# Cosine attention on one core: fourteen pairs of heads turned by transfers, a sixth key chunk off ScalarE, twelve K scalings on VectorE

## The chip, the cores and the metric

The kernel runs on one core of one Trainium2 chip. The metric is the device time of one execution in microseconds, the median of several executions. The engines are TensorE (PE in the profile, its weight loads PEld), VectorE (DVE), ScalarE (ACT), GpSimd (POOL) and SyncE (SP, which here only issues transfers). Each runs its own list of instructions in order, and waits on semaphores.

## The reference

```python
# batch 8, heads 12, seq 512, dim 64, float32; tau 0.1
Q_norm = Q / (norm(Q, axis=-1) + 1e-10)
K_norm = K / (norm(K, axis=-1) + 1e-10)
scores = einsum('bhqd,bhkd->bhqk', Q_norm, K_norm) / tau
weights = exp(scores - max(scores));  weights /= sum(weights)
out = einsum('bhqk,bhkd->bhqd', weights, V)
```

The kernel needs no maximum: the scores of normalised rows lie between -10 and 10.

## The kernel before, in words

The 96 heads are worked off as 48 pairs. A pair's Q, K and V are 256 KB each. The steps of pair s, by the names in the code (a step's name is also its key in the program's table):

- LD and LV load Q, K and V (SP issues them); VC casts V to bf16 (GpSimd).
- SQ squares (GpSimd), SSQ and RED sum the squares of K (TensorE, then VectorE); BN and RED(s,0) take the statistics of Q on VectorE. NEW works out the reciprocal roots, for a group of up to four pairs at once (pairs 36 to 39, 40 to 43 and 44 to 47 are such groups).
- SCL(s,0) scales Q on VectorE, SCL(s,1) scales K: on GpSimd, or on VectorE for the pairs in `K_ON_DVE`. Result: tile qn, bf16, 128x512 each.
- TR(s,0), TR(s,1) turn Q and K on TensorE, four 128x128 transposes each, into the bank tps; EVA copies both to qt on VectorE.
- SCO(s,c) makes the scores of key chunk c (128 keys, both heads, two matmuls 64x128 by 64x512) in one half of the bank set scps. EXP(s,c) on ScalarE makes the weights of the chunk, 128x1024, one instruction. So a chunk's scores can be made when the exponential two chunks earlier has ended.
- PV(s,h,i) multiplies weights and V for head h and query block i (four matmuls). RCP and NRM divide by the sums on VectorE (one NRM of 128x512 for a pair, two of 128x256 for pairs with an off chunk and the last ones), ST stores. PV of the next pair writes the bank that NRM reads, so it waits for that NRM.

Five chunks have no exponential on ScalarE, the "off" chunks of the table `OFF`: chunk 3 of pairs 25, 33, 40 and 44, and chunk 2 of pair 47. Theirs is a polynomial: SCX(s,h) makes the scores of head h (one matmul) in the bank tps, X(s,h,0) and X(s,h,1) on VectorE read them into xp and xz, and Y(s,0) to Y(s,4), five steps on GpSimd, give the weights. There is one bank, so SCX(s,1) waits for X(s,0,1); there is one set of xp, xz and xw, so the next off chunk's X waits for the last Y of this one.

Rings of buffers: 15 for Q and K, 10 for V, 4 for qn, 4 for qt, 4 for the weights, 8 for the output.

The order of the work on each engine is written out in the table `ORDER` (from line 883): a list of numbers for each engine, each number the place of a step in the order in which the program was made up. Nothing is moved at run time; a step that waits holds up all that stands behind it on its engine. The waits themselves come from the needs that each step names.

The code has a second way of turning Q and K, used for pairs from `TURN_FROM` on: TD(s), one transposing transfer from qn to qt for Q and K together (line 555), issued by SP. It needs both scalings of the pair, and the scores of pair s-4, whose qt it overwrites. With `TURN_FROM = 99` no pair has it.

Of the kernel before, what the change touches and what calls it, by code (L numbers as in the profile page):

```python
# [5 lines left out]
ALU = mybir.AluOpType  # L6
# [103 lines left out]
def bass_cosine_similarity_attention_kernel(  # L110
# [10 lines left out]
    NT = SEQ // 128  # L121
# [48 lines left out]
    P = Program(nc)  # L170
# [179 lines left out]
    def pair(s):  # L350
# [164 lines left out]
        for w in range(2):  # L515
# [29 lines left out]
            def tr(e, w=w):  # L545
                for t in range(NT):
# [5 lines left out]
                  [("SCL", s, w), *(([("EVA", s - 1, 0)] if s - 1 in BY_HEAD else evas(s - 1)) if s > 1 else [("EVA", 0, 0, 0), ("EVA", 0, 0, 1)]), "eye"]  # L552
                  + [freed(*u) for u in turn_user.get(s - 1, [])[-1:]], tr)
# [21 lines left out]
    def turned(s):  # L575
        return s >= TURN_FROM

    last_eva = min(TURN_FROM, NP) - 1

# [32 lines left out]
    def freed(s, h):  # L612
        return ("Y", s, h, 3) if in_psum(s) else ("X", s, h, 1)

    def poly(s, c, at):
# [6 lines left out]
        for h in range(2):  # L622
            users = turn_user[turns[h]]
            before = [freed(*users[users.index((s, h)) - 1])] if users.index((s, h)) else []
            if turns[h] is None:
                before += [("SCL", i, w) for i in range(NP - 12, NP) for w in range(2)]
            elif prev:
                before.append(freed(prev[-1], 1))

            def sco(e, h=h):  # L630
# [3 lines left out]
            P.add(("SCX", s, h), "pe", "sco1", at + h, [*evas(s), *evas(min(turns[0], last_eva))] + before, sco)  # L634
            lift = LIFT_P if here else LIFT
            b_ps = x_ps if turns[h] is not None else nx_ps
            P.add(("X", s, h, 0), "dve", "x1", at + h, [("SCX", s, h)] + (exps(held[-1], off_of[held[-1]]) if held and not here else []),
# [3 lines left out]
                  (lambda e, h=h, b_ps=b_ps: e.scalar_tensor_tensor(out=yz[:, h, :], in0=b_ps, scalar=lift * UNIT - a0, in1=y_low[h], op0=ALU.add, op1=ALU.subtract)) if here else  # L641
                  (lambda e, h=h: e.scalar_tensor_tensor(out=xz[:, h, :], in0=xp[:, h, :], scalar=a0 - lift * UNIT, in1=x_ps, op0=ALU.add, op1=ALU.subtract)))  # L642
            if not here:
# [3 lines left out]
                      lambda e, h=h, b_ps=b_ps: e.scalar_tensor_tensor(out=et[s % R_ET][:, c, h, :], in0=yz[:, h, :], scalar=a1, in1=b_ps, op0=ALU.add, op1=ALU.mult)]  # L647
            for j, (step, need) in enumerate(zip(halves, ([("X", s, h, 1)] + [("Y", i, 4) for i in held[-1:]] + [cast_of(i) for i in range(NP - 8, NP)], [("Y", s, i, 1) for i in range(2)],
                                                          [("Y", s, h, 2)] + [key("PV", s - R_ET, i, NT - 1) for i in range(2)]))):
                P.add(("Y", s, h, j + 1), "pool" if j == 1 else "dve", "sqp" if j == 1 else "x1", at + 2 + 0.5 * h + 0.8 * j, need, step)  # L650
# [162 lines left out]
OFF = {(25, 3): (25, 25), (33, 3): (33, 33), (40, 3): (40, 40), (44, 3): (44, 44), (47, 2): (47, None)}  # L813
# [19 lines left out]
TURN_FROM = 99  # L833
# [4 lines left out]
OFF_ON_POOL = ((25, 3), (33, 3), (40, 3), (44, 3), (47, 2))  # L838
OFF_ON_BOTH = ()
X_ON_POOL = ()  # L840
K_ON_DVE = (1, 2, 3, 4, 9)
# [33 lines left out]
def slack(s, most):  # L875
# [133 lines left out]
```

## Time and profile before

| | |
|---|---|
| median of 3 runs | 185.53 us (185.46 to 185.81) |
| the profiled execution | 185.63 us, span from first to last instruction 183.9 us |
| granted TensorE clock | 1.000 |
| busy: TensorE, VectorE, ScalarE, GpSimd | 173.0, 172.9, 176.9, 163.8 us |
| the 16 DMA engines | full until about 124 us, when the last loads land; then stores alone |

How to read the rows: a group has line, engine, operation, output<-input, shapes and count, then the busy time in us, the mean of one in ns, and the idle time of the engine just before them with what ended it. A timeline row has start, duration, engine, line, operation, and in brackets an idle time before it. A windows row has the stretch, its length, and the busy us (with instruction counts) of PE, PEld, DVE, ACT and POOL, then the clock, the DMA share and GB/s. The durations of neighbouring VectorE or ScalarE instructions overlap a little, so what one costs its engine is the distance from its start to the next one's.

Lines: L538 is SCL, L547 TR, L570 EVA, L413 BN and the Q half of RED, L435 SSQ, L692 SCO, L716 and L707 EXP, L631 SCX, L639 and L642 X, L656, L657 and L662 Y, L741 and L778 PV, L760 and L789 RCP, L762 and L791 NRM, L725 VC.

### The profile page before, as it was taken

The page shows a single profiled execution, that of the slowest core. Times are in us where ns is not written, and L with a number is a line of the kernel's source. Part 1 is how long each engine was busy: PE and PEld are TensorE (multiplying, and loading weights), DVE is VectorE, ACT ScalarE, POOL GpSimd, SP SyncE. Part 2 cuts the span into 40 slices and gives each one's busy share as a digit, 9 for nine tenths or more (in the row PEclk, how much of TensorE's full clock was granted, in tenths as well). Part 3 has the DMA queues.
Part 4 walks back from the last instruction along what each step waited for, and adds up shares of the span by engine and source line. Part 5 has one row for each costly group of instructions (what it writes and reads, how often), then busy time and mean ns, then how long its engine had stood idle before and what let it go on. Part 6 is the DMA issues. An engine that isn't in the chain of part 4 may idle for free.

```text
span 183.9 us, 6826 instructions
## 1 busy us (share of the span) xinstructions
PE 173.0 (94%) x2738; PEld 109.9 (60%) x2738; DVE 172.9 (94%) x622; ACT 176.9 (96%) x205; POOL 163.8 (89%) x153
## 2 busy tenths in 40 slices
PE   7989999999999999999999899999899999899993
PEld 2546666657666666666755566656466656556562
DVE  2799999999999999999999999999999999997995
ACT  5799999999999999999999999999999999999992
POOL 4699999839989999996999999999999999998960
PEclk9999999999999999999999999999999999999999
DMA  5999999999999999999999999995115213013134
GB/s 162 331 356 346 349 350 356 380 375 384 379 376 377 379 383 379 383 378 375 357 372 383 370 383 380 377 323 190 61 59 193 96 62 114 5 65 110 57 132 157
DMA packets 52479, 50.77 MB, mean 276 GB/s; under 512 B 3296, under 2 KB 52448, under 8 KB 52448
## 3 DMA queue, kind: packets, MB, share of 16 engines
q1 hardware_dynamic: 52016, 50.05, 79.8%
q8 instruction: 21, 0.34, 0.8%
q10 hardware_dynamic: 432, 0.30, 0.5%
q14 instruction: 10, 0.08, 0.1%
HBM read 37.75 MB, written 12.58 MB: 274 GB/s over the span
## 4 chain that ended last, share of the span: by engine, by line
ACT 69%; DVE 11%; PE 10%; POOL 5%; issue 2%; DMA 1%; POOLq 1%; DVEq 0%
ACT et L716 68%; PE oops L741 3%; PE scps L692 3%; POOL xw L657 2%; DVE ob L762 2%; DVE qn L538 1%; PE tps L547 1%; DMA qk<-in_Q_dram 1%; DVE qt L570 1%; POOL et L657 1%; DVE xp L639 1%; PE oops L435 1%; DVE xs L284 1%; DVE xz L642 1%; DVE et L647 1%
## 5 line engine op out<-in xcount | busy, mean ns | idle before, releaser
L716 ACT ACTIVATE et<-scps 128x1024 bf16<-128x1024 f32 (+1 forms) x188 | 171.1, 1073 | 1.3 <-PE scps L692 1.2
L692 PE MATMUL scps<-qt 64*128 64x512 bf16 x374 | 73.7, 386 | 4.5 <-ACT et L716 3.6
L741 PE MATMUL oops<-vb,et 128*128 128x65 bf16 x1504 | 70.3, 194 | 0.9 <-DVE ob L762 0.8
L741 PEld LDWEIGHTS oops<-vb,et 128*128 128x128 bf16 x1504 | 54.5, 97 | 26.4 <-issue 16.0
L538 POOL TENSOR_TENSOR qn<-qk,rk 128x512 bf16<-128x512 f32 x42 | 43.5, 1043 | 7.4 <-DVE rk L482 4.1
L538 DVE TENSOR_TENSOR qn<-qk,nps 128x512 bf16<-128x512 f32 x52 | 34.7, 678 | 0.6 <-ACT nps L474 0.6
L394 POOL TENSOR_TENSOR sq<-qk 128x512 bf16<-128x512 f32 x34 | 34.9, 1040 | 0.0
L762 DVE TENSOR_TENSOR ob<-oops,rd 128x256 f32<-128x256 f32 (+1 forms) x64 | 34.3, 542 | 0.3
L547 PE MATMUL tps<-ident,qn 128*128 128x128 bf16 x376 | 32.5, 220 | 0.6 <-DVE qn L538 0.3
L570 DVE COPY qt<-tps 128x1024 bf16<-128x1024 bf16 x47 | 32.0, 681 | 0.8 <-PE tps L547 0.7
L413 DVE BATCH_NORM_STATS2 st<-qk 128x6 f32<-128x128 f32 x136 | 31.7, 282 | 0.0
L692 PEld LDWEIGHTS scps<-qt 64*128 64x128 bf16 x374 | 18.0, 92 | 21.1 <-ACT et L716 8.5
L547 PEld LDWEIGHTS tps<-ident,qn 128*128 128x128 bf16 x376 | 21.4, 98 | 11.6 <-issue 5.2
L725 POOL TENSOR_SCALAR vb<-vf 128x1024 bf16<-128x1024 f32 (+1 forms) x29 | 26.2, 910 | 0.3
L397 POOL TENSOR_TENSOR sq<-qk 128x1024 bf16<-128x1024 f32 x10 | 18.8, 1893 | 0.1
L435 PE MATMUL oops<-sq,ident 128*128 128x64 bf16 x320 | 16.0, 193 | 0.0
L435 PEld LDWEIGHTS oops<-sq,ident 128*128 128x128 bf16 x320 | 11.9, 98 | 4.1 <-issue 3.1
L760 DVE RECIPROCAL rd<-oops 128x4 f32<-128x4 f32 (+1 forms) x64 | 11.4, 186 | 1.0 <-PE oops L741 0.4
L657 POOL TENSOR_TENSOR xw<-xw,xz 128x1024 f32<-128x1024 f32 x4 | 9.4, 2358 | 0.3
L657 POOL TENSOR_TENSOR et<-xw,xp 128x1024 bf16<-128x1024 f32 x4 | 8.5, 2133 | 0.2
L448 DVE TENSOR_REDUCE nps<-oops 128x8 f32<-128x64 f32 x38 | 8.1, 213 | 0.1
L657 POOL TENSOR_TENSOR xw<-xz 128x1024 f32<-128x1024 f32 x4 | 7.6, 1893 | 0.7 <-DVE xz L642 0.7
(76 smaller groups left out, 111.4 us busy)
## 6 DMA issues: line engine op xcount, KB each, us to landing
vf<-in_V_dram SPq DMA_DIRECT2D x48, 256.0 KB, 6.4
out_dram<-ob SPq DMA_DIRECT2D x47, 256.0 KB, 6.3
qk<-in_Q_dram SPq DMA_DIRECT2D x46, 256.0 KB, 6.4
qk<-in_K_dram SPq DMA_DIRECT2D x46, 256.0 KB, 6.5
qk<-in_Q_dram SPq DMA_DIRECT2D x4, 128.0 KB, 3.0
qk<-in_K_dram ACTq DMA_DIRECT2D x2, 128.0 KB, 2.8
qk<-in_K_dram SPq DMA_DIRECT2D x2, 128.0 KB, 3.2
out_dram<-ob SPq DMA_DIRECT2D x1, 128.0 KB, 1.7
```

What stands on the lines that cost most here:

```text
L394: lambda e: e.tensor_tensor(out=sqf[:, 8 * DIM :], in0=data[:, 8 * DIM :], in1=data[:, 8 * DIM :], op=ALU.mult))
L413: last = e.bn_stats(out=st[:, g % R_X, c8 + 4 * h + t : c8 + 4 * h + t + 2, :].rearrange("p g x -> p (g x)"), in_=rows[:, t : t + 2].rearr ...
L435: last = e.matmul(out=o_ps[bank][:, at : at + 64], lhsT=ident[:, :], rhs=sq[iqs][:, 8 * w : 8 * w + 8, 8 * k : 8 * k + 8], start=(k == 0), ...
L538: lambda e, w=w, r=r: e.tensor_tensor(out=qn[iqn][:, w].rearrange("p t h d -> p h t d"), in0=qk[iq][:, w].rearrange("p h (t d) -> p h t d" ...
L547: last = e.transpose(t_ps[:, w, t, :], qn[iqn][:, w, t].rearrange("p h d -> p (h d)"), ident[:, :])
L570: lambda e, ws=ws: e.tensor_copy(out=qt[iqt][:, ws, :, :].rearrange("p w t x -> p (w t x)"), in_=t_ps[:, ws, :, :].rearrange("p w t x -> p ...
L657: mul = lambda o, x, y: lambda e: e.tensor_tensor(out=o, in0=x, in1=y, op=ALU.mult)
L692: last = e.matmul(out=sc_ps[:, 2 * b + h, :], lhsT=qt[iqt][64 * h : 64 * h + 64, 1, c, :], rhs=qt[iqt][64 * h : 64 * h + 64, 0, :, :], sta ...
L716: lambda e, c=c, b=b, hs=hs: e.activation(out=et[iet][:, c, hs[0] : hs[-1] + 1, :], in_=sc_ps[:, 2 * b + hs[0] : 2 * b + hs[-1] + 1, :], f ...
L725: return e.tensor_scalar(out=vb[:, ib // 2, :, ib % 2 : ib % 2 + n, :, 0:DIM].rearrange("p c r h d -> p (r h) c d"), in0=vf[:, iv : iv + n ...
L741: last = e.matmul(out=o_ps[h][:, 65 * t : 65 * t + 65], lhsT=et[iet][:, c, h, 128 * t : 128 * t + 128], rhs=vb[:, s % R_VB // 2, c, s % 2, ...
L762: lambda e, hs=hs, grid=grid: e.tensor_tensor(out=ob[io][:, hs], in0=grid[:, :, :, 0:DIM], in1=rd[io][:, hs, :].unsqueeze(3).to_broadcast( ...
```

## The change

- `TURN` names the pairs 34 to 47: their TR and EVA steps are gone (28 and 14), and 14 transposing transfers TD stand in SP's list.
- `OFF` has a sixth chunk, (38, 3), its polynomial on GpSimd: one EXP less, two SCX, four X and five Y more; pair 38's RCP and NRM come in two halves, and the scales of its group are made for the polynomial.
- `K_ON_DVE` has pairs 36 to 47 more: twelve SCL(s,1) go from GpSimd to VectorE. All pairs of their groups are then on VectorE, so NEW needs no step more.
- The needs are written for any set of turned pairs (`eva_by`); an off chunk's SCX waits for the last EVA before it. A variant `IN_PLACE` is added and empty.
- The orders of SP, GpSimd, VectorE and TensorE are new from about pair 12 on; ScalarE's loses EXP(38,3).

```diff
+            P.add(("TR", s, w), "pe", "tr", T0 - PERIOD + 0.9 * TR_AT[w],
+                  [("SCL", s, w), *(([("EVA", s - 1, 0)] if s - 1 in BY_HEAD else evas(eva_by(s - 1))) if s > 1 else [("EVA", 0, 0, 0), ("EVA", 0, 0, 1)]), "eye"]
...
     def turned(s):
-        return s >= TURN_FROM
+        return s in TURN
-    last_eva = min(TURN_FROM, NP) - 1
+    last_eva = max(s for s in range(NP) if not turned(s))
+    def eva_by(s):
+        return max(i for i in range(s + 1) if not turned(i))
...
-            P.add(("SCX", s, h), "pe", "sco1", at + h, [*evas(s), *evas(min(turns[0], last_eva))] + before, sco)
+            P.add(("SCX", s, h), "pe", "sco1", at + h, [*evas(s), *evas(eva_by(turns[0]))] + before, sco)
...
-OFF = {(25, 3): (25, 25), (33, 3): (33, 33), (40, 3): (40, 40), (44, 3): (44, 44), (47, 2): (47, None)}
+OFF = {(25, 3): (25, 25), (33, 3): (33, 33), (38, 3): (38, 38), (40, 3): (40, 40), (44, 3): (44, 44), (47, 2): (47, None)}
-TURN_FROM = 99
+IN_PLACE = ()
+TURN = tuple(range(34, 48))
 TURN_AT = 10
-OFF_ON_POOL = ((25, 3), (33, 3), (40, 3), (44, 3), (47, 2))
+OFF_ON_POOL = ((25, 3), (33, 3), (38, 3), (40, 3), (44, 3), (47, 2))
-K_ON_DVE = (1, 2, 3, 4, 9)
+K_ON_DVE = (1, 2, 3, 4, 9, 36, 37, 38, 39, 40, 41, 42, 43, 44, 45, 46, 47)
```

The parts of the new lists that the text below speaks of, with the numbers resolved into names:

```
TensorE  ... SCO(35,2) SCO(35,3) SCX(38,0) PV(34,0,0) PV(34,0,1) PV(34,0,2) PV(34,1,0) PV(34,0,3) PV(34,1,1)
         PV(34,1,2) SSQ(42,1) PV(34,1,3) SCX(38,1) SCO(36,0) SCO(36,1) PV(35,0,0) ...
         ... PV(40,0,2) PV(40,0,3) SCO(43,0) ...     (PV(40,h,3) needs Y(40,4))
         ... PV(47,2,2) PV(47,2,3) PV(47,1,3) PV(47,0,0) PV(47,0,1) PV(47,0,2) PV(47,0,3)
VectorE  ... SCL(38,0) SCL(38,1) BN(42) SCL(36,1) NEW RCP(32) RED(40,1) NRM(32) SCL(36,0) SCL(39,0) SCL(37,1)
         SCL(37,0) NEW RCP(33,1) RCP(33,0) RED(41,1) NRM(33,0) NRM(33,1) X(38,0,0) X(38,0,1) RCP(34)
         RED(42,1) NRM(34) X(38,1,0) NEW X(38,1,1) ...
         ... NRM(37) X(40,0,0) NEW X(40,0,1) SCL(42,1) X(40,1,0) RCP(38,0) RED(46,1) X(40,1,1) ...
GpSimd   ... Y(38,0) to Y(38,4) SQ(47) VC(40) Y(40,0) to Y(40,4) VC(42) VC(44) VC(46) Y(44,0) to Y(44,4) ...
SP       ... LV(44) TD(34) TD(35) LV(41) TD(38) TD(36) TD(37) ST(28) ST(30) ST(32) TD(39) TD(40) TD(41)
         LV(40) LV(46) TD(42) LV(47) LV(45) ST(31) ST(34) TD(43) LV(43) TD(44) ST(36) LV(42) TD(45) ...
```

In TensorE's list before, two of pair 34's PV stand ahead of SCO(35,3), four between it and SCO(36,0), and two with the SSQ behind that.

More of the change, by code (lines that the diff above doesn't have):

```diff
@@ L551, in pair @@
             P.add(("TR", s, w), "pe", "tr", T0 - PERIOD + 0.9 * TR_AT[w],
-                  [("SCL", s, w), *(([("EVA", s - 1, 0)] if s - 1 in BY_HEAD else evas(s - 1)) if s > 1 else [("EVA", 0, 0, 0), ("EVA", 0, 0, 1)]), "eye"]
-                  + [freed(*u) for u in turn_user.get(s - 1, [])[-1:]], tr)
+                  [("SCL", s, w), *(([("EVA", s - 1, 0)] if s - 1 in BY_HEAD else evas(eva_by(s - 1))) if s > 1 else [("EVA", 0, 0, 0), ("EVA", 0, 0, 1)]), "eye"]
+                  + [freed(*u) for i in range(eva_by(s - 1), s) for u in turn_user.get(i, [])[-1:]], tr)
         if turned(s):
@@ L627, in poly @@
             elif prev:
-                before.append(freed(prev[-1], 1))
+                before.append(freed(prev[-1], max(i for i in range(2) if OFF[prev[-1], off_of[prev[-1]]][i] is not None)))
             def sco(e, h=h):
@@ L632, in sco @@
                                 rhs=qt[s % R_QT][64 * h : 64 * h + 64, 0, :, :], start=True, stop=True)
-            P.add(("SCX", s, h), "pe", "sco1", at + h, [*evas(s), *evas(min(turns[0], last_eva))] + before, sco)
+            P.add(("SCX", s, h), "pe", "sco1", at + h, [*evas(s), *evas(eva_by(turns[0]))] + before, sco)
             lift = LIFT_P if here else LIFT
             b_ps = x_ps if turns[h] is not None else nx_ps
-            P.add(("X", s, h, 0), "dve", "x1", at + h, [("SCX", s, h)] + (exps(held[-1], off_of[held[-1]]) if held and not here else []),
+            P.add(("X", s, h, 0), "dve", "x1", at + h, [("SCX", s, h)] + [("Y", i, h, 3) for i in prev if here and in_psum(i)] + (exps(held[-1], off_of[held[-1]]) if held and not here else []),
                   (lambda e, h=h, b_ps=b_ps: e.tensor_scalar(out=yp[:, h, :], in0=b_ps, scalar1=-MIDDLE, scalar2=BIG + lift * UNIT, op0=ALU.add, op1=ALU.add)) if here else
@@ L640, in poly @@
             P.add(("X", s, h, 1), "dve", "x1", at + h, [("X", s, h, 0)],
-                  (lambda e, h=h, b_ps=b_ps: e.scalar_tensor_tensor(out=yz[:, h, :], in0=b_ps, scalar=lift * UNIT - a0, in1=y_low[h], op0=ALU.add, op1=ALU.subtract)) if here else
+                  (lambda e, h=h, b_ps=b_ps: e.scalar_tensor_tensor(out=b_ps if s in IN_PLACE else yz[:, h, :], in0=b_ps, scalar=lift * UNIT - a0, in1=y_low[h], op0=ALU.add, op1=ALU.subtract)) if here else
                   (lambda e, h=h: e.scalar_tensor_tensor(out=xz[:, h, :], in0=xp[:, h, :], scalar=a0 - lift * UNIT, in1=x_ps, op0=ALU.add, op1=ALU.subtract)))
@@ L647, in poly @@
                       lambda e, h=h, b_ps=b_ps: e.scalar_tensor_tensor(out=et[s % R_ET][:, c, h, :], in0=yz[:, h, :], scalar=a1, in1=b_ps, op0=ALU.add, op1=ALU.mult)]
+            if s in IN_PLACE:
+                halves = [lambda e, h=h, b_ps=b_ps: e.tensor_tensor(out=yz[:, h, :], in0=b_ps, in1=b_ps, op=ALU.mult),
+                          lambda e, h=h, b_ps=b_ps: e.scalar_tensor_tensor(out=b_ps, in0=b_ps, scalar=-a2, in1=y_two[h], op0=ALU.add, op1=ALU.mult),
+                          halves[2]]
+                for j, (step, need) in enumerate(zip(halves, ([("X", s, h, 1)], [("Y", s, h, 1)], [("Y", s, h, 2)] + [key("PV", s - R_ET, i, NT - 1) for i in range(2)]))):
+                    P.add(("Y", s, h, j + 1), "dve" if j else "pool", "x1" if j else "sqp", at + 2 + 0.5 * h + 0.8 * j, need, step)
+                continue
             for j, (step, need) in enumerate(zip(halves, ([("X", s, h, 1)] + [("Y", i, 4) for i in held[-1:]] + [cast_of(i) for i in range(NP - 8, NP)], [("Y", s, i, 1) for i in range(2)],
```

109 rows, old and new, of the table ORDER are left out of this document.

## The prediction

> **What bounds the kernel now.** I read the page's busy times and slices first, then the chain, then the groups with shapes kept apart, then the timelines of single engines from 126 us on, where the change lies.
>
> ```profile
> span 183.9 us, 6826 instructions
> PE 173.0 (94%) x2738; PEld 109.9 (60%) x2738; DVE 172.9 (94%) x622; ACT 176.9 (96%) x205; POOL 163.8 (89%) x153
> ...
> DVE  2799999999999999999999999999999999997995
> ACT  5799999999999999999999999999999999999992
> ...
> 9.09 124.45 ACT et L716 x137
> ...
> L716 ACT ACTIVATE et<-scps 128x1024 bf16<-128x1024 f32 x184 | 169.1, 1084 | 0.1
> L538 POOL TENSOR_TENSOR qn<-qk,rk 128x512 bf16<-128x512 f32 x42 | 43.5, 1043 | 7.4 <-DVE rk L482 4.1 <-DVE nps L482 3.2
> L538 DVE TENSOR_TENSOR qn<-qk,nps 128x512 bf16<-128x512 f32 x52 | 34.7, 678 | 0.6 <-ACT nps L474 0.6
> L547 PE MATMUL tps<-ident,qn 128*128 128x128 bf16 x376 | 32.5, 220 | 0.6 <-DVE qn L538 0.3 <-DVE xz L642 0.3
> L570 DVE COPY qt<-tps 128x1024 bf16<-128x1024 bf16 x47 | 32.0, 681 | 0.8 <-PE tps L547 0.7
> ```
>
> ScalarE is the bound: its exponentials idle 0.1 us in all, and the chain stays on them from 9 us to 133 us. One costs 169.1/184 = 0.92 us. But VectorE is nearly as full. From where the two orders part (VectorE's list, pair 12's normalising at about 59 us) to 136 us:
>
> ```profile
> 58.00:136.00 78.00, 74.78 (x1227) 47.84 (x1227) 77.63 (x291) 78.00 (x86) 74.42 (x67) 1.00 0.97 334
> ```
>
> The third busy time is VectorE: 77.63 of 78.00 us. An order that gives it more to do before some point reaches that point later by all of it but 0.37 us. So each edit has two questions: does ScalarE lose an instruction, and what must VectorE have done when ScalarE's next scores are due?
>
> **The change part by part.**
>
> *Pair 38's sixth chunk leaves ScalarE:* one 128x1024 exponential less, -0.92 us, if nothing makes ScalarE wait.
>
> *Q and K of pairs 34 to 47 turned by transfers:* off TensorE go 14x8 transposes (0.55 to 0.59 us a pair), which gain nothing by themselves, as TensorE is not the bound; off VectorE go 14 copies (L570).
>
> *K of pairs 36 to 47 scaled on VectorE:* 12 scalings of 1043 ns leave GpSimd and come to VectorE. GpSimd gets pair 38's five polynomial steps (8.7 us, below), so it ends about 4 us lighter. VectorE's costs, by the starts of neighbours, since their durations overlap:
>
> ```profile
> 133.16 0.68 DVE L762 TENSOR_TENSOR ob<-oops,rd 128x512 f32<-128x512 f32 x1
> 133.76 0.68 DVE L538 TENSOR_TENSOR qn<-qk,nps 128x512 bf16<-128x512 f32 x1
> 134.36 0.48 DVE L413 BATCH_NORM_STATS2 st<-qk 128x6 f32<-128x128 f32 x2
> 134.76 0.67 DVE L538 TENSOR_TENSOR qn<-qk,nps 128x512 bf16<-128x512 f32 x1
> ...
> 136.13 0.40 DVE L762 TENSOR_TENSOR ob<-oops,rd 128x256 f32<-128x256 f32 x1
> ...
> 136.54 0.42 DVE L762 TENSOR_TENSOR ob<-oops,rd 128x256 f32<-128x256 f32 x1
> ...
> 147.45 0.68 DVE L570 COPY qt<-tps 128x1024 bf16<-128x1024 bf16 x1
> 148.05 0.68 DVE L538 TENSOR_TENSOR qn<-qk,nps 128x512 bf16<-128x512 f32 x1
> 148.68 0.69 DVE L639 TENSOR_SCALAR xp<-tps 128x512 int16<-128x512 f32 x1
> 149.41 0.69 DVE L642 SCALAR_TENSOR_TENSOR xz<-xp,tps 128x512 f32<-128x512 int16 x1
> 150.16 0.21 DVE L760 RECIPROCAL rd<-oops 128x8 f32<-128x8 f32 x1
> ```
>
> A scaling takes 0.60 us (133.76 to 134.36), a copy of the turned pair 0.60 (147.45 to 148.05), two statistics 0.40 (134.36 to 134.76), an X step of an off chunk 0.73. In all VectorE loses 14x0.60 = 8.4 us and gets 12x0.60 + 4x0.73 = 10.1 us: +1.7 us on a full engine.
>
> *The orders:* here the change decides itself. TensorE's new list has, after SCO(35,3): SCX(38,0), pair 34's eight PV steps with one sum of squares (SSQ) among them, SCX(38,1), and only then SCO(36,0), on which ScalarE's next exponential hangs. SCX(38,1) writes the bank that X(38,0,1) on VectorE reads, so it waits for it; and VectorE has X(38,0,0) and X(38,0,1) behind both normalisings of pair 33. TensorE waits in that place before too, once:
>
> ```profile
> 163.78 0.39 PE L631 MATMUL tps<-qt 64*128 64x512 bf16 x1 [0.34 <-DVE xz L642]
> ```
>
> When is VectorE there? Up to pair 33's first normalising (136.13 before) the new list has eight operations more: five scalings (38 K, 36 K, 39 Q, 37 K, 37 Q; 5x0.60), two of statistics (2x0.40) and one short step (0.10), 3.9 us; and two copies less (34, 35; 1.2 us). That is +2.7: 138.8, or 138.4 if it uses up all 0.37 us that were idle. The second normalising and the first X follow at 0.33 each, the second X 0.73 later, and takes 0.69: X(38,0,1) ends 2.1 us on, at 140.5 to 140.9. Then SCX(38,1) and SCO(36,0):
>
> ```profile
> 135.20 0.40 PE L435 MATMUL oops<-sq,ident 128*128 128x64 bf16 x8
> 135.43 0.29 PE L741 MATMUL oops<-vb,et 128*128 128x65 bf16 x4
> ...
> 137.25 0.39 PE L692 MATMUL scps<-qt 64*128 64x512 bf16 x2
> 137.57 0.66 PE L741 MATMUL oops<-vb,et 128*128 128x65 bf16 x16
> 138.25 0.39 PE L692 MATMUL scps<-qt 64*128 64x512 bf16 x2
> ```
>
> A score step takes 0.32 us (137.25 to 137.57), so SCO(36,0) is done at 141.2 to 141.6. ScalarE needs it when EXP(35,3) ends:
>
> ```profile
> 175.65 3.93 ACT L716 ACTIVATE et<-scps 128x1024 bf16<-128x1024 f32 x4
> 179.47 1.15 ACT L707 ACTIVATE et<-scps 128x512 bf16<-128x512 f32 x3
> ```
>
> The four from 175.65 are EXP(46,2), (46,3), (47,0), (47,1). From EXP(36,0) to EXP(46,1) there are 40 (ten pairs of four, two chunks fewer in 40 and 44, two more of 46), so EXP(36,0) begins at 175.65 - 40x0.92 = 138.85 before. ScalarE stands for 2.4 to 2.8 us. Even with no VectorE wait at all, TensorE's own list from SCO(35,3) (due at 137.0, two exponentials earlier) to SCO(36,0) holds four steps of 0.32, eight PV of 0.17 (16 matmuls are four, 0.68 to the next start) and an SSQ of 0.23 (135.20 to 135.43): 2.9 us, end at 139.9, a stall of 1.0. So the stall lies between 1.0 and 2.8; I take 2.4, the low end of VectorE's own rows, since short VectorE waits of before vanish when it is the late one. ScalarE makes none of it up.
>
> *GpSimd's second chain* says the same. The off chunks share xp, xz and xw: X(40) waits for the last Y of 38, X(44) for that of 40.
>
> ```profile
> 152.52 1.89 POOL L657 TENSOR_TENSOR xw<-xz 128x1024 f32<-128x1024 f32 x1
> ...
> 160.06 2.14 POOL L657 TENSOR_TENSOR et<-xw,xp 128x1024 bf16<-128x1024 f32 x1
> ...
> 165.85 1.89 POOL L657 TENSOR_TENSOR xw<-xz 128x1024 f32<-128x1024 f32 x1 [0.66 <-DVE xz L642]
> ...
> 172.52 2.13 POOL L657 TENSOR_TENSOR et<-xw,xp 128x1024 bf16<-128x1024 f32 x1
> ```
>
> Five steps take 8.8 us (165.85 to 174.65). X(38) ends 2.4 us after X(38,0,1) (pair 34's reciprocal, reduction, normalising 0.83; two X 1.42; a short step), at 142.9 to 143.3; Y(38) 151.7 to 152.1; X(40) takes 3.8 as before (148.68 to 152.52), Y(40) ends at 164.3 to 164.7, before at 162.2. SCO(43,0) stands behind a PV that needs it: 165.0 at best, where EXP(43,0) fell due at 163.7 (175.65 - 13x0.92), less 0.92, plus the stall of 2.4 = 165.2. Towards the end Y(44) comes 2.2 us later, but V(46)'s cast (one of 1.06 us) is moved out of the chain: +1.1, less than ScalarE's +1.5. So this chain adds nothing, and would alone cost as much.
>
> *SP's queue:* TD(36) stands behind TD(38), which waits for SCO(34,3), about 133.7; SCL(36,0) on VectorE ends later, at 136.7: it follows pair 32's normalising, which began at 133.16 and has 2.3 us more ahead of it in the new list (three scalings and four statistics more, two copies less). So TD(36) leaves at 136.7 and has until SCX(38,1) is through, 140.9: 4.2 us. No row shows a transposing transfer. Nearest are 256 KB transfers, on a quiet queue and on a full one:
>
> ```profile
> DMA to landing us min/median/max: 1.6/2.1/4.8
> ...
> qk<-in_Q_dram SPq DMA_DIRECT2D x46, 256.0 KB, 6.4
> ```
>
> The queue is quiet from 130 us on, so I take 2.1: hidden. At 6.4 it adds 2.2 us. Later ones have three pairs of lead, as qt has four buffers. Stores and the V loads of 40 to 47 queue behind the TDs; V(42) stands behind TD(44), which waits for pair 44's scalings; GpSimd casts it after Y(40), 164 us, so it is covered while these scalings end by 160. [...]
>
> *The end:* PV(47,0), 16 matmuls, now comes after the last exponential's PV, and its 256-wide normalising last.
>
> ```profile
> 179.71 0.74 PE L778 MATMUL oops<-vb,et 128*128 128x65 bf16 x17 [0.28 <-DVE ob L762]
> ...
> 181.38 0.35 DVE L791 TENSOR_TENSOR ob<-tps,rd 128x192 f32<-128x192 f32 x1
> ```
>
> Before, the last exponential ends at 180.62 and the last normalising at 181.73, 1.1 us on. Now it is 0.1 + 16x0.044 + a reciprocal and hand-overs 0.25 + 0.42 = 1.5: +0.4 (0 if those PVs' bank gates anyway).
>
> **Sum:** -0.92 + 2.4 + 0.35 = +1.8 us of span. The profiled execution took 185.63 us, 1.7 us around the span, and is 0.1 us above the median of 185.53. So 185.53 + 1.8 = 187.3. Ends: with TensorE's list alone (1.0, no tail) 185.6; with 2.8 and 0.4, and 0.3 more at pair 39, where PV(38) waits for pair 37's normalising, 188.1; with a 6.4 us transfer some 2 us more.
>
> **Rivals.** *The exponential's time is simply saved (faster):* VectorE is in time, its short steps hiding in its own gaps, and TensorE's steps run closer than counted, so that the stall stays under 0.55 us (0.92 - 0.37): 184.6 to 185.1. It decides at X(38,0,1): an end by 138.7. For it: TensorE and GpSimd get slack, and V(46)'s cast leaves the last chain. Against: VectorE's 77.63 of 78.00. Chance 0.13. *It evens out:* a stall of about one exponential, from TensorE's list alone: 185.2 to 185.9; for it the 2.9 us counted above, against it the wait for X. Chance 0.12. *Transfers set the pace:* if a transposing transfer holds the queue as long as a load does from issue to landing, each of 14 pairs takes 6.4 instead of 4x0.92 = 3.68 us: +38 us, 223 us. It decides at 3.7 us each. For it: packets could be small; against: 2.1 us for a store. Chance 0.05. *A late first transfer* (4.3 to 6.4 us, not pacing): 188 to 189.5, chance 0.07. My forecast has the rest, 0.63.
>
> [...]
>
> **How the numbers follow.** 0.2% is 0.37 us, about what can be told from no change. Faster 0.13; same 0.1; slower 0.77 (the last of "evens out" among it). The range 185.1 to 188.8 leaves out the faster case and the transfers' pacing, about 0.18. My own case alone is 186.4 to 188.1.
>
> **What would show it.** Right: ScalarE's exponentials with one idle stretch of about 2.4 us near 139 to 141, released by TensorE's scores; there TensorE waits at L631 for VectorE's xz; VectorE busy throughout to that point; transposing transfers landing in 2 to 3 us; POOL idle shares larger. Wrong: ScalarE without idle time (the saving stands), VectorE reaching pair 33's normalising before 137, scores waiting for qt by transfer in every pair (pacing), or the stall much shorter because X(38) comes earlier.

## The result, and the profile after

The changed kernel takes 192.12 us (median of 4 runs, 190.62 to 192.85); the kernel before took 185.53 us on the same chip. The ratio is 1.034, 95% interval [1.028, 1.041]: +6.3 us where +1.8 had been forecast, outside the range given. The direction was right and the size was not. The profiled execution took 192.85 us, the slowest of the four. Ratios, here and below, are of undisturbed runs, so they need not be those of the medians.

The page of the changed kernel, its busy times and three of its slice rows:

```profile
span 191.1 us, 6637 instructions
PE 171.9 (90%) x2626; PEld 105.8 (55%) x2626; DVE 172.4 (90%) x626; ACT 177.1 (93%) x204; POOL 160.4 (84%) x146
...
ACT  4799999999999999999999999999929999769992
...
PEclk9999999999999999999999999999969999658999
DMA  5999999999999999999999992975782399967546
```

Two things are new: ScalarE has holes at 139 to 143 us and after 165, and TensorE's granted clock, 1.000 throughout before, falls in the same two places. The ScalarE group and its timeline (start, length, what, count, in brackets the wait ahead and who ended it):

```profile
L726 ACT ACTIVATE et<-scps 128x1024 bf16<-128x1024 f32 (+1 forms) x187 | 171.2, 1063 | 7.7 <-PE scps L702 7.5
```

```profile
59.18 80.14 ACT L726 ACTIVATE et<-scps 128x1024 bf16<-128x1024 f32 x87
142.92 23.07 ACT L726 ACTIVATE et<-scps 128x1024 bf16<-128x1024 f32 x25 [3.60 <-PE scps L702]
167.63 1.02 ACT L726 ACTIVATE et<-scps 128x1024 bf16<-128x1024 f32 x1 [1.64 <-PE scps L702]
169.15 2.12 ACT L726 ACTIVATE et<-scps 128x1024 bf16<-128x1024 f32 x2 [0.50 <-PE scps L702]
171.77 13.38 ACT L726 ACTIVATE et<-scps 128x1024 bf16<-128x1024 f32 x14 [0.50 <-PE scps L702]
```

One wait of 3.60 us ahead of EXP(36,0), where 2.4 was forecast, and a second group of 2.64 us ahead of EXP(42,3), (43,0) and (43,2), where none was. With small ones 7.7 us in all (1.3 before). The exponentials are busy 171.2 us, one fewer than before in the same time: one that starts after its predecessor has ended takes 1.02 us instead of 0.92, and there are more of these now. From the last exponential's end (187.37) to the end is 3.7 us, 0.45 more than before.

What EXP(36,0) waited for, in the chain (start, length, what held it):

```profile
134.26 4.93 DMA qt<-qn
...
139.24 0.39 PE tps L634
139.62 1.65 PE oops L751 x28
```

The chain leaves VectorE and enters a transposing transfer, TD(38), issued at 134.26 and landed 4.93 us later. The first instruction behind it is SCX(38,0), the score step of the sixth chunk. TensorE and VectorE around it:

```profile
136.95 0.89 PE L702 MATMUL scps<-qt 64*128 64x512 bf16 x4
139.24 0.39 PE L634 MATMUL tps<-qt 64*128 64x512 bf16 x1 [1.40 <-DMA qt<-qn]
139.56 1.72 PE L751 MATMUL oops<-vb,et 128*128 128x65 bf16 x28
...
141.86 0.60 PE L634 MATMUL tps<-qt 64*128 64x512 bf16 x1
```

```profile
137.64 0.75 DVE L772 TENSOR_TENSOR ob<-oops,rd 128x256 f32<-128x256 f32 x2
139.66 0.69 DVE L642 TENSOR_SCALAR xp<-tps 128x512 int16<-128x512 f32 x1 [1.26 <-PE tps L634]
140.39 0.69 DVE L645 SCALAR_TENSOR_TENSOR xz<-xp,tps 128x512 f32<-128x512 int16 x1
```

VectorE is not the late one: it had normalised pair 33 from 137.64 on and then waited 1.26 us for TensorE, which waited 1.40 us for the transfer, with all of pair 34's PV steps and SCO(36,0) queued behind. These PV steps are then slow, 28 matmuls in 1.65 us (before, 16 took 0.66, at a clock of 1.00), as TensorE's granted clock is 0.50 there: SCX(38,1) starts only at 141.86, straight behind them, though X(38,0,1) had ended at 141.08. The granted clock in two stretches (start and end, length, PE busy with its count, then PEclk, DMA share, GB/s):

```profile
139.75:143.00 3.25, 3.25 (x45) 0.50 0.97 292
163.75:173.25 9.50, 7.66 (x66) 0.50 0.67 183
```

The second group in the chain:

```profile
152.98 3.25 DMA vf<-in_V_dram
...
156.31 1.06 POOL vb L735
...
163.99 2.13 POOL et L667
...
166.23 0.82 PE oops L751 x12
```

V(40), behind TD(41) on SP's queue, lands at 156.23; GpSimd casts it, runs Y(40) until 166.12, and twelve PV matmuls follow, with SCO(42,3) behind them. Read like this, three things are late: a transfer, a load behind a transfer, and TensorE's clock.

But the step from Y(40) to those matmuls is a coincidence. By the list they are PV(40,0,0), PV(40,1,0) and PV(40,0,1), and none of them needs Y(40). Of GpSimd they need the cast alone, done at 157.4; they wait for NRM(39), which reads the bank that they write. On VectorE NRM(39) ended at 166.08, 0.04 us ahead of Y(40). It stood behind SCL(47,0), which writes the buffer that TD(43) reads (there are four qn buffers), and which waited for that transfer's landing (total, times, longest):

```profile
DVE qn L538 <- DMA qt<-qn: 2.2, 1, 2.2
```

So behind the second group stands a transfer again, TD(43). The runs show which of the late things were causes.

### The profile page after: what moved, and what is told of

The parts are those of the page before. It is cut to its first block, busy times and chain, and to the rows that moved or that the text cites. A ratio compares the mean times of both kernels' runs of the same rounds, so it can differ in the third digit from the quotient of the medians.

```text
span 191.1 us, 6637 instructions
## 1 busy us (share of the span) xinstructions
PE 171.9 (90%) x2626; PEld 105.8 (55%) x2626; DVE 172.4 (90%) x626; ACT 177.1 (93%) x204; POOL 160.4 (84%) x146
## 4 chain that ended last, share of the span: by engine, by line
ACT 52%; DVE 21%; PE 11%; DMA 7%; POOL 5%; issue 1%; SPq 1%; DVEq 0%; POOLq 0%
ACT et L726 51%; PE oops L751 5%; DVE qn L538 4%; DVE ob L772 4%; DVE st L413 3%; PE scps L702 3%; DMA qt<-qn 3%; POOL xw L667 2%; DMA vf<-in_V_dram 2%; DMA out_dram<-ob 1%; DMA qk<-in_Q_dram 1%; DVE qt L570 1%; POOL et L667 1%; DVE rd L770 1%; DVE xp L642 1%
## 5 line engine op out<-in xcount | busy, mean ns | idle before, releaser
L726 ACT ACTIVATE et<-scps 128x1024 bf16<-128x1024 f32 (+1 forms) x187 | 171.2, 1063 | 7.7 <-PE scps L702 7.5
L751 PE MATMUL oops<-vb,et 128*128 128x65 bf16 x1504 | 73.0, 197 | 3.4 <-POOL et L667 1.4
L538 DVE TENSOR_TENSOR qn<-qk,nps 128x512 bf16<-128x512 f32 x64 | 41.9, 676 | 2.9 <-DMA qt<-qn 2.2
L538 POOL TENSOR_TENSOR qn<-qk,rk 128x512 bf16<-128x512 f32 x30 | 30.8, 1042 | 6.4 <-DVE nps L482 4.1
L547 PE MATMUL tps<-ident,qn 128*128 128x128 bf16 x264 | 23.5, 221 | 0.1
L570 DVE COPY qt<-tps 128x1024 bf16<-128x1024 bf16 x33 | 22.3, 676 | 0.1
L547 PEld LDWEIGHTS tps<-ident,qn 128*128 128x128 bf16 x264 | 15.0, 98 | 8.3 <-issue 2.9
L667 POOL TENSOR_TENSOR xw<-xz 128x1024 f32<-128x1024 f32 x5 | 9.5, 1892 | 5.8 <-DVE xz L645 5.8
L667 POOL TENSOR_TENSOR xw<-xw,xz 128x1024 f32<-128x1024 f32 x5 | 11.8, 2355 | 0.4
L667 POOL TENSOR_TENSOR et<-xw,xp 128x1024 bf16<-128x1024 f32 x5 | 10.7, 2130 | 0.4
L642 DVE TENSOR_SCALAR xp<-tps 128x512 int16<-128x512 f32 x10 | 6.8, 684 | 2.9 <-PE tps L634 2.9
```

What stands on the lines that cost most here:

```text
L538: lambda e, w=w, r=r: e.tensor_tensor(out=qn[iqn][:, w].rearrange("p t h d -> p h t d"), in0=qk[iq][:, w].rearrange("p h (t d) -> p h t d" ...
L547: last = e.transpose(t_ps[:, w, t, :], qn[iqn][:, w, t].rearrange("p h d -> p (h d)"), ident[:, :])
L570: lambda e, ws=ws: e.tensor_copy(out=qt[iqt][:, ws, :, :].rearrange("p w t x -> p (w t x)"), in_=t_ps[:, ws, :, :].rearrange("p w t x -> p ...
L667: mul = lambda o, x, y: lambda e: e.tensor_tensor(out=o, in0=x, in1=y, op=ALU.mult)
L726: lambda e, c=c, b=b, hs=hs: e.activation(out=et[iet][:, c, hs[0] : hs[-1] + 1, :], in_=sc_ps[:, 2 * b + hs[0] : 2 * b + hs[-1] + 1, :], f ...
L751: last = e.matmul(out=o_ps[h][:, 65 * t : 65 * t + 65], lhsT=et[iet][:, c, h, 128 * t : 128 * t + 128], rhs=vb[:, s % R_VB // 2, c, s % 2, ...
```

## The experiments

Theory T: the places where an engine waits for a landing, and the clock that falls when TensorE waits, cost the difference. Rival V, the forecast's own: VectorE's load. Rival R2: transposing transfers slow everything. "Above" is (ratio - 1) x 185.6 us; "clock" is that of the profiled execution.

| kernel | median us | ratio to before, 95% | above, us | clock |
|---|---|---|---|---|
| changed | 192.12 | 1.034 [1.028, 1.041] | 6.3 | 0.963 |
| q6 | 190.26 | 1.024 [1.020, 1.028] | 4.5 | 0.973 |
| vload | 191.66 | 1.032 [1.028, 1.036] | 5.9 | 0.978 |
| all2 = q6 + vload | 189.47 | 1.020 [1.018, 1.022] | 3.7 | 0.982 |
| all3 = all2 + idle matmuls | 188.79 | 1.015 [1.012, 1.018] | 2.8 | 0.998 |
| qn6 = all2 + more qn buffers | 188.13 | 1.013 [1.010, 1.016] | 2.5 | 0.982 |
| stores = all2 + stores moved | 191.69 | 1.033 [1.029, 1.037] | 6.1 | 0.973 |
| fill | 193.99 | 1.043 [1.038, 1.048] | 8.0 | 0.980 |
| vload_fill | 191.97 | 1.034 [1.032, 1.036] | 6.3 | 0.994 |
| nooff | 191.92 | 1.033 [1.031, 1.035] | 6.1 | 0.972 |
| nooff2 | 191.40 | 1.028 [1.023, 1.033] | 5.2 | 0.982 |
| nooff3 | 191.34 | 1.031 [1.028, 1.034] | 5.8 | 0.998 |
| idletd | 185.71 | 0.9995 [0.998, 1.001] | -0.1 | 0.998 |
| u3 | 189.99 | 1.022 [1.016, 1.027] | 4.0 | 0.981 |
| u3_fill | 191.46 | 1.019 [1.012, 1.025] | 3.5 | 1.000 |
| konly | 191.08 | 1.029 [1.026, 1.032] | 5.4 | 1.000 |
| h | 199.45 | 1.071 [1.064, 1.077] | 13.1 | 0.946 |
| h_fill | 196.34 | 1.056 [1.052, 1.060] | 10.4 | 0.982 |
| q3_fill | 193.74 | 1.041 [1.035, 1.048] | 7.6 | 0.985 |

**The place of TD(38) (q6).** TD(38) overwrites the buffer of pair 34, of which there are four, and so waits for SCO(34,3). With six it needn't:

```diff
-RINGS = 15, 10, 6, 4, 4, 4, 8, 3, 16
+RINGS = 15, 10, 6, 4, 6, 4, 8, 3, 16
```

> The changed kernel with six buffers of turned Q and K in place of four, so that TD(38) no longer waits for the scores of pair 34; orders the same. Theory T: TD(38) leaves 0.8-1.2 us sooner, SCX(38,0) starts at 138.0-138.4 in place of 139.24, the wait ahead of EXP(36,0) shrinks by 0.6-1.5 us (by the upper end if TensorE's clock no longer falls there), time 189.5-191.5. Rival V (VectorE's scalings set the stall): TD(38)'s place is worth under 0.3 us, 191.6-192.5.

It left at 132.8, SCX(38,0) started at 137.4, the wait ahead of EXP(36,0) shrank from 3.60 to 1.11 us, by more than T had said. Rival V's "under 0.3" is out. The place is worth some 1.8 us (the two intervals just touch). Part of that is the clock, which stays at 1.00 there in q6; the next run divides the two.

**V's loads ahead (vload).**

```diff
 SP: ST(28) ST(30) ST(32)
+    LV(40) LV(43) LV(42)
     TD(39) TD(40) TD(41)
-    LV(40)
     LV(46) TD(42) ... TD(43)
-    LV(43)
     TD(44) ST(36)
-    LV(42)
```

> The changed kernel with V's loads of pairs 40, 43 and 42 moved on SP's queue ahead of the transposing transfers of 39 to 41. Theory Q (the chain of waits read literally: GpSimd's 2.22 us of waiting for the load of V(40) delays Y(40) and with it the exp of pair 43): 189.5-190.3. Theory X (VectorE's X(40,1,1), which ends at 156.91, is late next, 0.46 us ahead of where the cast ended): 191.3-192.4, GpSimd waiting for VectorE instead, Y(40,0) at 156.9-157.0.

GpSimd and ScalarE after it:

```profile
153.22 1.06 POOL L735 TENSOR_SCALAR vb<-vf 128x1024 bf16<-128x1024 f32 x1
156.00 1.89 POOL L667 TENSOR_TENSOR xw<-xz 128x1024 f32<-128x1024 f32 x1 [1.71 <-DVE xz L645]
...
141.81 23.19 ACT L726 ACTIVATE et<-scps 128x1024 bf16<-128x1024 f32 x25 [2.38 <-PE scps L702]
```

The cast is done 3 us sooner, Y(40) then waits 1.71 us for VectorE's X(40), and the time is the one that theory X gave; theory Q, the chain read literally, is out. Both theories took for granted that ScalarE waits for Y(40) in the end. It doesn't: SCL(47,0) still waits 2.0 us for TD(43), and the same twelve PV matmuls start 0.14 us after NRM(39).

This run also has TD(38) as late as the changed kernel has (SCX(38,0) starts at 139.27), but a clock of 1.00 at that place, and its wait ahead of EXP(36,0) is 2.38 us. So, by these three traces, of the 3.60 us about 1.2 go with the half clock and 1.3 with TD(38); 1.1 are left in q6.

**Both (all2), with idle matmuls (all3, and these alone, fill).** Idle matmuls are ident on ident into the transposes' bank, put ahead of TensorE's waits:

```diff
+P.fill = lambda e, n: [e.matmul(out=x_ps[:, 0:64], lhsT=ident[:, :],
+                       rhs=ident[:, 0:64], start=True, stop=True) for _ in range(n)][-1]
```

> As the three together, but without the idle matmuls: six buffers of turned Q and K, and V's loads of 40, 43 and 42 ahead. Theory T: with the two queue places mended TensorE still waits, so its clock falls at least once, most likely between 158 and 168; 189.3-190.3, that is 0.5-1.5 us more than with the idle matmuls (188.79). Rival V (the clock is only an effect and costs nothing by itself): 188.5-189.1, equal to the three together.

> All three together: six buffers of turned Q and K, V's loads of 40, 43 and 42 ahead, idle matmuls in TensorE's waits (256 of them). Theory T: 187.9-188.9, clock 1.00, one stall of 1.3-1.8 us left at EXP(36,0), which waits for TD(36) and for SCX(38,1) and so in the end for VectorE's scalings. Rival R2 (the transposing transfers slow every other transfer, whatever the queue's order): over 190. Theory that the three places were all: below 186.

> The changed kernel with 284 idle matmuls (ident on ident, 64 columns, into the transposes' PSUM bank, where it has no reader) put into TensorE's queue where it waits from 126 us on; nothing else differs. Theory T (TensorE lost the turning, waits more, its granted clock falls to 0.50 from 139.6 to 143.0 and from 163.5 to 173.6, and that stretches the two stalls): the clock stays at 1.00, the wait ahead of EXP(36,0) shrinks from 3.6 to 2.0-2.6 us, those from EXP(42,3) to EXP(44,0) from 3.1 together to about 1; time 188.5-189.7. Rival V (VectorE's load and the queues set the time, the clock is only their effect): 191.5-192.8, the stalls as they were. Rival W (matmuls in the way): over 192.8.

Both times of all2 and all3 came out as T said: 3.7 and 2.8 us above, intervals apart (the stall left in all3 is 1.02 us, below its 1.3 to 1.8). ScalarE in all2:

```profile
140.76 23.20 ACT L726 ACTIVATE et<-scps 128x1024 bf16<-128x1024 f32 x25 [1.12 <-PE scps L702]
165.16 1.02 ACT L726 ACTIVATE et<-scps 128x1024 bf16<-128x1024 f32 x1 [1.19 <-PE scps L702]
166.68 16.04 ACT L726 ACTIVATE et<-scps 128x1024 bf16<-128x1024 f32 x17 [0.50 <-PE scps L702]
```

The idle matmuls alone (fill) missed: the first wait fell to 1.74 us, below the 2.0 to 2.6 expected, but the kernel got slower. Its chain:

```profile
157.73 6.76 DMA qt<-qn
...
165.79 0.70 DVE ob L772
...
166.62 0.53 PE oops L751 x12
```

Here the chain names NRM(39) itself: TD(43) took 6.76 us to land, SCL(47,0) waited for it, and NRM(39), on which PV(40) hangs, stood behind. It is the place behind the second group, only later. In all2 it is still there, as the waits of VectorE show:

```profile
DVE qn L538 <- DMA qt<-qn: 1.8, 1, 1.8
```

**The place of TD(43) (qn6).** Six qn buffers, on top of all2:

```diff
-RINGS = 15, 10, 6, 4, 6, 4, 8, 3, 16
+RINGS = 15, 10, 6, 6, 6, 4, 8, 3, 16
```

> As the kernel with six buffers of turned Q and K and V's loads of 40, 43 and 42 ahead (189.47, 3.7 us above the kernel before), and also six buffers of scaled Q and K (qn) in place of four, so that VectorE's SCL(47,0) no longer stands 1.8 us for TD(43) to land, with pair 39's normalising behind it. Theory Q (every wait for a landing is a cost of its own): 0.5-1.3 us less, 2.4-3.2 above the kernel before. Theory V (what is left is VectorE's and GpSimd's own chain): within 0.4 us of it.

3.7 falls to 2.5 us, and EXP(42,3) waits 0.19 instead of 1.19:

```profile
140.53 23.20 ACT L726 ACTIVATE et<-scps 128x1024 bf16<-128x1024 f32 x25 [1.13 <-PE scps L702]
163.92 1.02 ACT L726 ACTIVATE et<-scps 128x1024 bf16<-128x1024 f32 x1 [0.19 <-PE scps L702]
165.44 2.12 ACT L726 ACTIVATE et<-scps 128x1024 bf16<-128x1024 f32 x2 [0.50 <-PE scps L702]
168.06 13.92 ACT L726 ACTIVATE et<-scps 128x1024 bf16<-128x1024 f32 x15 [0.50 <-PE scps L702]
```

It is the best form of the change that was run. Three edits that touch no work, only buffers and places, take 3.8 of the 6.3 us back. No form of the change was faster than the kernel before.

**Do the transfers cost by being there (idletd)?** The kernel before, with 14 such transfers that nobody waits for, a constant tile into spare tiles:

```diff
+P.add(("TX", i), "sp", "td", ..., lambda e: e.dma_start_transpose(out=xt[i % 4], in_=xq))
 SP: ... ST(30) +TX(0) ST(31) +TX(1) ... ST(43) +TX(13)
```

> The kernel before, with 14 transposing transfers of the change's size (128x1024 bf16) added that nobody waits for: a constant tile is turned into four spare tiles, one behind each output store of pairs 30 to 43 on SP's queue. Everything else, the turning on TensorE included, stays. Theory T (the transfers cost by what waits for them, not by being there): 185.5-186.3, clock 1.00. Rival R2 (they slow the other transfers or the engines): over 187.

185.71 against 185.73 us. R2 in that form is out: where nobody waits for them, such transfers cost nothing here. Their issues on SP and their landings:

```profile
L806 SPq DMA_TRANSPOSE xt<-xq x14: 1267/1288/2043, 126.5 to 174.1; - x14
...
DMA to landing us min/median/max: 3.2/3.5/5.1
```

**Do other transfers slow them (stores)?** On top of all2, four ready stores moved between TD(39) and TD(41) from their places further down:

```diff
 SP: TD(39)
+    ST(31) ST(33) ST(34)
     TD(40)
+    ST(35)
     TD(41)
```

> The changed kernel with six buffers of turned Q and K, V's loads of 40, 43 and 42 ahead, no idle matmuls (189.47 so far), and the stores of pairs 31, 33, 34 moved on SP's queue behind TD(39), that of 35 behind TD(40), where their data has long been there. Theory Q (each store or load behind a late transfer is one more place that holds VectorE or TensorE up: NRM(43) waits for the store of 35): 188.5-189.3. Theory V (what is left is VectorE's and GpSimd's own chain): 189.2-189.9, no change.

Both theories missed: 2.4 us slower. SP's queue, the chain and TensorE:

```profile
144.16 2.06 SPq L776 DMA_DIRECT2D out_dram<-ob  x3
146.44 2.27 SPq L556 DMA_TRANSPOSE qt<-qn  x1
```

```profile
146.44 6.26 DMA qt<-qn
```

```profile
152.74 0.60 PE L634 MATMUL tps<-qt 64*128 64x512 bf16 x1 [2.50 <-DMA qt<-qn]
```

TD(40), which landed after 3.04 us in all2, took 6.26 behind three stores, and SCX(40,0) held TensorE for 2.50 us. The three stores themselves landed after 5.9 to 6.5 us, where three issued from 139.2 to 140.4, ahead of V's loads, took 2.4 to 3.1. So in this run stores and transposing transfers slowed each other, and here, unlike in idletd, TensorE waited for one.

**Is it the sixth chunk (nooff; nooff3 with the repairs and idle matmuls; nooff2 = stores without it)?** Pair 38's chunk 3 gets its exponential back:

```diff
-OFF = {..., (33, 3): (33, 33), (38, 3): (38, 38), (40, 3): (40, 40), ...}
+OFF = {..., (33, 3): (33, 33), (40, 3): (40, 40), ...}
```

> The changed kernel without the sixth key chunk off ScalarE: pair 38's chunk 3 has its exp again, SCX(38), X(38) and Y(38) are gone; turning, K on VectorE and the orders of the rest stay. ScalarE has 0.92 us more work, VectorE 2.7 us less, GpSimd 8.6 us less. Theory T: with no SCX(38) ahead of it SCO(36,0) waits only for the transfer TD(36), which left at 135.59 and landed at 140.03: a wait of 1.2-1.8 us at EXP(36,0) in place of 3.6; Y(40) starts as soon as X(40) is there, no wait over 1 us at pair 43; 188.0-189.8. Rival V (VectorE's load alone): with 2.7 us less of it the wait at EXP(36,0) is under 0.5 us, 186.3-187.3. Rival R2 (any transposing transfer slows the rest): over 190.5.

> The changed kernel without the sixth chunk off ScalarE, with the three repairs (six buffers of turned Q and K, V's loads ahead, 294 idle matmuls); pair 38's chunk 3 has its exp again. Theory T (turning and K on VectorE cost by what waits for a transfer, the sixth chunk is worth its 0.92 us less what SCX(38) holds up): 188.3-189.6, a wait of 1.0-1.8 us at EXP(36,0), which is TD(36)'s landing alone. If the sixth chunk were the cause of what is left: 186.0-187.0.

> The kernel just above without the sixth chunk: pair 38's chunk 3 has its exp again, SCX(38), X(38), Y(38) are gone. No idle matmuls stand in the way here. Theory T (EXP(36,0) then waits for TD(36)'s landing, about as long as it waited for SCX(38,1); ScalarE has 0.92 us more): 0.3-1.3 us above the kernel with the sixth chunk. Rival (the sixth chunk's work on VectorE and GpSimd is what is left of the loss): 0.8 us or more below it.

Against its own partner nooff is -0.2 us with overlapping intervals, nooff2 -0.9 with overlapping ones, where T had said above and its rival 0.8 or more below; nooff3 was 3.0 us slower than all3, and why is open: its idle matmuls stand in other places, and some waited for VectorE (1.1 us in all). My 188 to 190 for nooff failed: its wait at EXP(36,0) was 1.28 us as forecast (TD(36)'s landing), but four more of 0.5 to 0.94 us stayed behind it. The chunk's own worth stays open; it is not what carries the loss.

**Each other part alone (u3: turning; konly: K on VectorE; h: both),** with orders laid anew from the durations before, which need not be the best, so each is an upper bound; and with idle matmuls (u3_fill, h_fill, and q3_fill, the whole change laid anew).

```diff
 u3     TURN = 34..47, K_ON_DVE = (1, 2, 3, 4, 9),            no (38, 3)
 konly  TURN = (),     K_ON_DVE = (1, 2, 3, 4, 9, 36 .. 47),  no (38, 3)
 h      TURN = 34..47, K_ON_DVE = (1, 2, 3, 4, 9, 36 .. 47),  no (38, 3)
```

> The kernel before with one part of the change alone: Q and K of pairs 34 to 47 turned by transfers (six buffers of turned Q and K), K on GpSimd, no sixth chunk; orders from 108 us laid anew around it, so that by measured durations no wait over 0.5 us is left. Theory T: the transfers keep up; TensorE, without 112 turning matmuls, falls to half clock for one or two stretches of 3.4 us: 185.9-188.0. Rival R2 (the transfers set the pace): over 189. No cost at all: 185.4-185.8.

> The same, with 181 idle matmuls in TensorE's waits from 120 us on. Theory T: clock 1.00, time 185.5-186.8 and at least 0.4 us below the one without them where that one's clock falls. Rival (the clock costs nothing): equal within 0.3 us.

> The kernel before with K of pairs 36 to 47 scaled by VectorE, and nothing else of the change: turning on TensorE and copied by VectorE, no sixth chunk, orders from 108 us laid anew. VectorE has 7.1 us more work in a stretch where it was busy 77.6 of 78 us. Theory V (VectorE's load costs by itself, which the change's transfers relieve by 8.4 us of copies): 188.3-189.5, TensorE's clock 1.00, waits spread over many exps under 0.8 us each. Rival (VectorE has room): below 186.5.

> Turning by transfers and K on VectorE for pairs 36 to 47, without the sixth chunk off ScalarE, six buffers of turned Q and K, and all the queues' orders from 100 us on laid anew so that by measured durations no wait over 0.4 us is left. Theory T: nothing in the two moves costs time by itself, but TensorE is left with too little work and its clock falls at times: 186.5-189.0. Rival V (VectorE is too full): over 189.5. Rival R2 (the transfers): over 189.5, with transfers landing after more than 5 us. Neither: 185.6-186.4.

> The same kernel as the one before it in this call, with 190 idle matmuls in TensorE's waits. Theory T: its clock stays at 1.00 and the time falls to 185.7-186.6, at least 0.7 us below the kernel without them. Rival (the clock costs nothing): equal within 0.3 us.

> The whole change with six buffers of turned Q and K, orders from 108 us laid anew, and 197 idle matmuls. Theory T: with the queue places and the clock mended VectorE's load is left (K's scalings and X(38) on top of a full engine), 187.5-189.0, waits of 1-2 us in all and an end 1-2 us longer after the last exp. If VectorE's load were no cost: below 185.3.

All six came out above what T expected of them, or V in konly. K's scalings on VectorE alone cost 5.4 us at a clock of 1.00: VectorE's load does cost there, as V says, though no run tells it from the new order. Turning alone costs 4.0, at a clock of 1.00 still 3.5 (this ratio rests on two runs). The times of u3 and h lie where R2 had been put (over 189, over 189.5), and h has landings over 5 us, as R2 said; idletd speaks against R2, but these two runs don't exclude it. In h the order laid anew crowded the first transfers: twelve loads and stores issued from 125.7 to 132.1 land up to 6.7 us later, and TD(34) behind them after 6.97. So its size may say more of that order than of the parts. Its pair with idle matmuls speaks for the clock: the runs behind the ratio of h have clocks of 0.954 to 0.963, those of h_fill 0.982 to 0.991, and h_fill is 2.7 us lower. But **vload_fill** says the other side:

> The changed kernel with V's loads of 40, 43 and 42 ahead, as in the run of those alone (191.66, four buffers of turned Q and K), and 298 idle matmuls in TensorE's waits. With those loads out of the way TD(44) landed at 164.08, so the late TD(44) that undid the idle matmuls alone is gone. Theory C (the clock is a cost of its own in the changed kernel): clock over 0.99, 188.8-190.3, at least 1.4 us below the run without idle matmuls. Rival (the clock's fall only fills waits): 191.2-192.

At 0.994 it is no faster than vload. One reason can be seen:

```profile
137.68 1.11 PE L219 MATMUL tps<-ident 128*128 128x64 bf16 x32
138.72 0.39 PE L634 MATMUL tps<-qt 64*128 64x512 bf16 x1
```

Here TD(38) had landed at 137.26, and SCX(38,0) stood behind 32 idle matmuls until 138.72. So the clock's own worth in the changed kernel isn't settled: 0.9 us from all2 to all3, 2.7 from h to h_fill, 0.5 with overlapping intervals from u3 to u3_fill, none from vload to vload_fill, and worse from the changed kernel to fill. The changed kernel's own four runs do fall in order by it (190.62 us at 0.982, 191.75 at 0.973, 192.49 at 0.970, 192.85 at 0.963), which doesn't say which of the two follows from the other.

## Why the prediction was wrong, step by step

**ScalarE loses 0.92 us:** an exponential is gone, but no run could show it as time.

**VectorE reaches pair 33's normalising at 138.4 to 138.8:** it came at 137.64. The load was counted about 1 us too high at this place. X(38,0,1) was late in the changed kernel for TD(38)'s sake, and even so SCX(38,1) did not wait for it but for the slow PV steps. With TD(38) out of the way (all2) the step can be measured by itself:

```profile
139.38 0.69 DVE L645 SCALAR_TENSOR_TENSOR xz<-xp,tps 128x512 f32<-128x512 int16 x1
```

```profile
140.12 0.39 PE L634 MATMUL tps<-qt 64*128 64x512 bf16 x1 [0.16 <-DVE xz L645]
```

X(38,0,1) ends at 140.07 (forecast 140.5 to 140.9) and the wait at EXP(36,0) is 1.12 us, near the low end that TensorE's list alone gave (1.0), not 2.4. The step's mechanism was there and its size twice too large: X(38,0,1) came 0.4 us sooner than the forecast's low end, and ScalarE came to this place 0.8 later (EXP(35,3) ends at 139.64, where EXP(36,0) had been due at 138.85).

**SP's queue: "so I take 2.1: hidden". This is the step that failed.** Two errors in it. Needs were missed: the text followed TD(36) and SCO(36,0), and named TD(38) only as what stands ahead; but SCX(38,0), first in the list that the forecast itself wrote down, reads what TD(38) turns; and SCL(47,0) overwrites what TD(43) reads. And the price was that of the wrong neighbour: 2.1 us is a quiet store. (The last loads do not land at 124 us before, as the table there has it, but at 128.7 and, two more of V, at 142.2 and 142.8; the store of 4.8 us in the forecast's row was issued behind these two.) The changed kernel's transfers:

```profile
L556 SPq DMA_TRANSPOSE qt<-qn x14: 1232/1233/1865, 126.4 to 175.2; - x14
...
DMA to landing us min/median/max: 3.1/3.7/4.9
```

SP issues each for 1.23 us and it lands after 3.1 to 4.9. In other runs some come to the forecast's bound of 6.4 for a full queue (6.26 in stores, 6.76 in fill). "Later ones have three pairs of lead" held for the scores of their own pair, but not for VectorE, which must have the source tile back, nor, in stores, for SCX(40,0), which TensorE runs early. q6 and qn6 price the step: 1.8 and 1.2 us, where the forecast had 0.

**V's loads behind the transfers, "covered":** V(40) was late, and GpSimd waited 2.22 us for it, but no run shows it reaching ScalarE: vload is 0.4 us lower, within the scatter.

**GpSimd's second chain "adds nothing":** it came out so. In all2 Y(40) ended at 163.74, sooner than the 164.3 to 164.7 forecast. In all3 the PV matmuls ahead of SCO(42,3) start while Y(40) still runs (until 163.79), released by NRM(39):

```profile
161.65 2.14 POOL L667 TENSOR_TENSOR et<-xw,xp 128x1024 bf16<-128x1024 f32 x1
```

```profile
163.48 0.53 PE L751 MATMUL oops<-vb,et 128*128 128x65 bf16 x12 [0.16 <-DVE ob L772]
```

So the waits at EXP(42,3) and behind it were not this chain's. That it "would alone cost as much" was not tried.

**The end:** +0.45 us, forecast +0.35.

**Not in the forecast at all:** TensorE's clock. "Gain nothing by themselves" was said of the 112 transposes taken off TensorE; konly, which keeps them, has a clock of 1.00, u3, which drops them, of 0.98.

**The direction** came out right partly by luck. With the stall at the 1.1 us that was measured, the forecast's own sum is -0.92 + 1.1 + 0.45 = +0.6 us, close to its rival "it evens out"; what made the change clearly slower stood in the step that had been put at nothing.

**The rivals.** The nearest was the late first transfer (188 to 189.5, chance 0.07): right in kind, but for TD(36) and once, where TD(38) and TD(43) are late in turn. The transfers don't set the pace: TD(38), TD(36) and TD(37) land at 139.19, 140.03 and 141.18, about 1 us apart, where a pair has 3.68. A transposing transfer of the changed kernel lands after 3.1 to 4.9 us, against 2.8 to 4.1 us for the loads of V after 125 us in the same trace and 2.1 us (the median) for the quiet stores before.

What remains after the repairs, 2.5 us in qn6, is 1.1 us of the forecast's own stall at EXP(36,0), 1.2 at pairs 42 and 43 with TensorE's clock at 0.76 on average from 158 to 172, the longer end, and some 0.5 by which ScalarE is behind already when EXP(35,3) ends, less the saved exponential. How much of this rest would go with the clock was not tried.

## What to carry to other kernels

When work moves from an engine to a transfer, list every instruction that reads its target or reuses its source, in queue order on every engine, not only the consumer you have in mind: an early reader in an in-order queue (a score step run two pairs ahead, a scaling that wants its buffer back) turns a landing time into a stall of everything behind it. Take the landing time from the busiest neighbour in the trace and check what else stands in that queue; here two more buffers on either side gave 1.8 and 1.2 us, without another order. And when the chain of waits names a releaser, look in the program whether the waiting step needs it at all: two things that end 0.04 us apart are easily taken for each other, and the edit then mends the wrong one.

## What the runs showed of the hardware

In the changed kernel a 128x1024 transposing transfer between on-chip tiles held SP for 1.23 to 1.87 us and landed after 3.1 to 4.9. In idletd, where nothing waited for them, seven of 14 landed after 3.2 to 3.3 us, four after 4.7 to 5.1. What makes the difference wasn't found. The changed kernel scattered by 2.2 us, the kernel before by 0.35 on the same chip; that the landings do this is not shown (all2, which waits for them too, scattered by 0.7).

In the changed kernel TensorE's granted clock fell to 0.50 for 3.4 us (139.6 to 143.0) and for 10.2 us (163.5 to 173.7), after waits no longer than 1.4 us. The stretches of 3.4 us just before, and one that had no such effect (TensorE busy, then PEclk, DMA share, GB/s):

```profile
129.40:132.80 3.40, 2.26 (x39) 1.00 0.66 161
136.20:139.60 3.40, 1.89 (x30) 1.00 1.12 131
160.10:163.50 3.40, 2.05 (x22) 1.00 1.11 262
```

Busy 56% and 60% of the stretch was followed by half the clock, 66% was not. The busy share alone doesn't decide it: from 135 to 140 us TensorE was busy for 3.54 us in vload and for 3.47 in the changed kernel, and in vload the clock stayed at 1.00 until 160. The second fall came 20.5 us after the first had ended, six times the first one's length, and lasted three times as long. What sets these times is not shown.
